# The last block of down: order of its products, place of its transposes, numbering of two PSUM pairs

## The chip, the cores and the metric

The kernel runs on one core of one Trainium2 chip. The metric is the device time of one execution in microseconds (us). Before the change it is 999.88 us, the median of 3 runs (999.58 to 1000.47).

## What is computed

Two residual layers over 512 tokens of 1024 features in float32. Each layer adds a token mixer (layer 0: causal pooling, layer 1: dilated sliding-window attention) and then a SwiGLU; a final rmsnorm follows. What matters here is the SwiGLU and what reads its result:

```python
def swiglu(h, w_gate, w_up, w_down):
    g = jnp.einsum('bsd,df->bsf', h, w_gate)
    u = jnp.einsum('bsd,df->bsf', h, w_up)
    return jnp.einsum('bsf,fd->bsd', jax.nn.silu(g) * u, w_down)

def reference(x, ...):
    for i in range(DEPTH):
        h = rmsnorm(x, norm_mix[i])
        ...
        x = x + y
        h = rmsnorm(x, norm_ffn[i])
        x = x + swiglu(h, ffn_w_gate[i], ffn_w_up[i], ffn_w_down[i])
    return rmsnorm(x, norm_final)
```

`D_FF` is 2816. After layer 0's SwiGLU comes the attention mixer of layer 1; after layer 1's, the final norm and the output.

## The kernel before

Every float32 operand is split into a high part (a cast to float32r on ACT, line 170 for weights: `whi`) and a low part (the rest, a subtraction on DVE, line 174: `wlo`). A product is then three matmuls: high by high, high by low, low by high.

`ffn` computes the SwiGLU with seven products in place of eight (a two-by-two block scheme of Strassen's kind). The features of D_FF are cut into 11 groups (0 to 10) of 256. A group's gate and up come from seven products ("one", "quad"); its activations go into `u_of`. `down` multiplies them with `w_down` in three blocks of groups (`BLOCKS`); the last block, 2, holds groups 6 to 10. In a block, `z` numbers pairs of groups: z = 0 is groups 6 and 7, z = 1 groups 8 and 9, z = 2 group 10 alone. Group 10 keeps its activations in the tiles `t2` and `t3` (high and low; rows of the profile without numbers say `t`), filled in two parts: two slots after quad 10's product 5 (`first_half`), five after its product 6 (`second_half`).

A product of `down` takes, per z, both token halves t and both groups c: 12 matmuls of 512 columns for z = 0 or 1, 6 for z = 2, so 30 in all (line 817). It sums into a pair of PSUM banks. PSUM has four such pairs, opened as `ffpairs`: two that alternate between groups and blocks (list `A`), `Q` (pair2) and `C` (pair3). In block 2, with `accs = (p, r, p, q, p, r, p)`, products 0, 2, 4 and 6 sum into the same pair `p`, 1 and 5 into `r` (which is `C`), 3 into `q` (which is `Q`). Product 0 is copied from `p` to `q` (line 832, ACT) and product 2 is added on top of it. After each product `flush` adds the pair to the residual stream `x` (line 840, DVE) or subtracts it (line 842); only then may the next product on that pair start (0 and 2 share one sum, which starts once). After product 4 the second token block is subtracted once more, for product 6, whose second token block goes to banks of its own.

When both halves of a block of 128 tokens are complete, `closed` squares them (line 323, ACT) and multiplies by the gain (332, DVE); `norm.prepare` scales by the inverse root (338 to 342, then 351 on ACT). After layer 0 the blocks are turned for attention: `turn_block` issues 8 transposes (line 357, PE), then casts (360, ACT) and low parts (361, DVE) into `h`. Blocks 2 and 3 are turned inside `ffn`, into `r` and `q`; the rest in attention. There `by_halves` starts on tiles of a PSUM pool whose four banks are those of the two pairs in `A`, bank 0 first, and needs `h` of blocks 2 and 3 first (lines 263 to 265; features in eight chunks).

PE's order is the order of the code (`manual_schedule`). The other engines' order is set by a scheduler with priorities, statically. Weights go through a queue in the order of `PLAN`: a load on SP's queue into one of 5 `wraw` tiles, in some cases a second one summed onto it by POOL's queue (138, 179), then the split into one of 5 pairs of tiles, up to four items ahead. Products 1, 2 and 5 have no load of their own for all of it: they reuse three `vraw` tiles, and for block 2 the operand of product 5 is that of product 2 plus a POOL DMA (line 179), issued once product 2's split has read the tile.

Of the kernel before, what the change touches and what calls it, by code (L numbers as in the profile page):

```python
# [51 lines left out]
def _plan():  # L52
    first = lambda n: [("quad", n, 0)] if n in PAIRED else []
    down = lambda b, i, *zs: ("down", b, i, zs or tuple(range((len(BLOCKS[b]) + 1) // 2)))
    steps = TWO + [("one", 2, i) for i in range(6)] + first(3) + [("one", 2, 6)]
    for n in PAIRED:
        steps += [("quad", n, i) for i in USED]
        ends = [("quad", n, 5), ("quad", n, 6)]
        if n in (3, 6):
            b = n // 3 - 1  # L60
            steps += [down(b, 0)] + ends + [down(b, i) for i in range(1, 6)] + first(n + 1) + [down(b, 6)]
        elif n == 10:
            steps += [down(2, 0, 0, 1)] + ends + [down(2, 1, 0, 1), down(2, 0, 2), down(2, 1, 2)]
            steps += [down(2, i) for i in (2, 4, 5, 3, 6)]
        else:
            steps += first(n + 1) + ends
    return steps


PLAN = _plan()  # L70
TOKENS = np.arange(S).reshape(J, R).T.reshape(-1)
BY_GROUP = [6, 7, 4, 5, 2, 3, 0, 1]
# [3 lines left out]
def trunk_kernel(ctx: ExitStack, tc: tile.TileContext, x_in, xT, gam, gains, consts, ident_d, w0, wT, w1, wv, w_down, out):  # L76
# [290 lines left out]
    def by_residue(b):  # L367

        n = P // R

        def places(h, half, tp):
            at = h[:, 4 * half : 4 * half + 4, :].rearrange("p c (r j) -> p c r j", r=R)
            return at[:, :, :, b * n : (b + 1) * n], tp.rearrange("p c (i r) -> p c r i", r=R)

        return places

    def turned(norm, shift, b, tps, order):

        hi, lo = tokens_at(shift)
        for half, tp in enumerate(tps):  # L380
            norm.turn(b, half, tp)
        for half, tp in enumerate(tps):
            (to_hi, src), (to_lo, _) = order(hi, half, tp), order(lo, half, tp)
            with tc.high_priority(URGENT):
                split(to_hi, to_lo, src)
# [51 lines left out]
    with ExitStack() as pctx:  # L437
# [64 lines left out]
        v, s, r = (tmp.tile([P, 4], F32, name=name) for name in ("v4", "s4", "r4"))  # L502
# [75 lines left out]
    def ffn(layer, norm, third, nxt):  # L578
# [8 lines left out]
        with ExitStack() as fctx:  # L587
# [193 lines left out]
            def late(b, what):  # L781
                js = slice((b - 2) * P, (b - 1) * P)
                tps = late_banks[b]
                at = lambda t: t[:, :, js]
                parts = lambda i: (at(T_hi[i]), at(T_lo[i]))
                if what == 1:
                    nc.vector.tensor_sub(at(t1r), at(t1r), tps[0])
                    split(*parts(0), at(t1r))
                    nc.scalar.copy(at(t3r), tps[0])
                elif what == 2:  # L790
                    nc.vector.scalar_tensor_tensor(at(t2r), at(t1r), -1.0, tps[1], op0=ALU.mult, op1=ALU.subtract)
                    split(*parts(1), at(t2r))
                elif what == 3:
                    nc.vector.tensor_sub(at(t3r), tps[1], at(t3r))
                    split(*parts(2), at(t3r))
                else:
                    split(at(block(h_hi, 1, 1)), at(block(h_lo, 1, 1)), tps[1])
                    nc.vector.scalar_tensor_tensor(at(t2r), at(t2r), -1.0, at(b21r), op0=ALU.mult, op1=ALU.subtract)
                    split(*parts(3), at(t2r))
# [49 lines left out]
            for at, (kind, n, i, *zs) in enumerate(PLAN[:-4]):  # L849
                if at in (0, 2):  # L850
                    b = 2 + at // 2
                    if b == 2:
                        late_banks[b] = third
                        norm.prepare(3, COLS)
                    else:
                        late_banks[b] = [r_tile(), by_four(mm.tile())]
                        for half in range(2):
                            norm.turn(b, half, late_banks[b][half])
                    late(b, 1)
                if at in (4, 6, 8):  # L860
                    for b in (2, 3):
                        late(b, at // 2)
                if kind == "down":
                    if n not in downs:
                        downs[n] = Down(n, A[0], C, Q)
                        A.reverse()
                    downs[n].product(i, *zs)
                    continue
                if kind == "quad" and i == 0:
                    groups[n] = Group(n, ct_common, (A[0], Q, C))  # L870
                    A.reverse()
                elif i == 0 and n not in groups:
                    groups[n] = Group(n, ct_common)
                groups[n].product(i, held={1: -2, 2: 1, 3: 1}.get(i, 0) if kind == "quad" else 0)
                if (n, i) == (2, 0):
                    with tc.high_priority(100), tc.issue_after(groups[2].kept.ins):
                        groups[1].second_half()
                    held.close()
                    late_u.append(open_pool("ffb", 2))
                if (n, i) == (1, 6):  # L880
                    fps.close()
                    mm.close()
                    fps.open("ffpairs", [P, 2, S], 1)
                    *A, Q, C = (fps.tile(f"pair{i}") for i in range(4))
                    A.reverse()


            final = layer == 1
# [3 lines left out]
            last = downs[2]  # L892
            p, r, _, q = last.accs[:4]

            def closed(half, blocks):
                for b in blocks:
                    norm.square(b, half, junk)
                    norm.gained(b, half)
# [15 lines left out]
            turn_block = lambda b, pair: turned(norm, 0, b, [by_four(pair[:, n, :]) for n in range(2)], by_residue(b))  # L914

            every = PLAN[-1][3]
            last.product(4, every)
            with tc.high_priority(URGENT):
                last.flush(6, p[:, 1:2, :], slice(1, 2))
            closed(1, (2, 3))  # L920
            last.product(5, every)
            closed(0, (2, 3))
            for b in (2, 3):
                ready_block(b)
            last.product(3, every)
            closed(0, (0, 1))
            if not final:
                turn_block(2, r)
            ws = last.operands(6, every)
            last.matmuls(6, ws, last.places(every, (0,)), lambda t: p[:, 0, :], False)  # L930
            with tc.high_priority(URGENT):
                last.flush(6, p[:, 0:1, :], slice(0, 1))
            closed(1, (0,))
            ready_block(0)
            if not final:
                turn_block(3, q)
            for n, cs in enumerate(HALVES if final else COLS[:1]):
                to = (A[0], r)[n][:, 0, : cs.stop - cs.start]
                last.matmuls(6, ws, last.places(every, (1,)), lambda t: to, True, cs)
                with tc.high_priority(URGENT):  # L940
                    last.flush(6, to.unsqueeze(1), slice(1, 2), cs)
                norm.square(1, 1, junk, 2 + n if final else None)
                norm.gained(1, 1, 2 + n if final else None)
# [5 lines left out]
        return norm  # L949

    norm = ffn(0, norm, third, 1)


    with ExitStack() as actx:
# [24 lines left out]
        def rope(ps, t, name):  # L979
            a = aw.tile([P, S], F32, name="ropea")  # L980
            sw = aw.tile([P, S], F32, name="ropeb")
            nc.vector.stream_shuffle(sw, ps, PARTNER)
            nc.vector.tensor_mul(a, ps, cosr)
            nc.gpsimd.tensor_mul(sw, sw, sinr)
            out = aw.tile([P, S], F32, name=name, bufs=3)

            if t >= 3:
                nc.vector.tensor_add(out, a, sw)
            elif name == "k":
                nc.vector.tensor_add(out.rearrange("p (b r i) -> p b r i", b=4, r=R), blocks_of(a), blocks_of(sw))  # L990
            else:
                by_r = lambda z: z.rearrange("p (r j) -> p r j", r=R)
                nc.vector.tensor_add(out.rearrange("p (j r) -> p r j", r=R), by_r(a), by_r(sw))
            return out
# [130 lines left out]
        for t in range(8):  # L1125
            pq = pqk[2 * t] if t < 2 else project(j_qk[2 * t], h_hi, h_lo)
            q = rope(pq, t, "q")
# [4 lines left out]
            if t in (4, 6):  # L1132
                first = (t, q, k)
# [166 lines left out]
        third = out_projection(j_wo, range(NC), m_hi, m_lo, norm, SHIFT, four, lambda: [sc_tile(), sc_tile()])  # L1300

    ffn(1, norm, third, 3)
    mm.close()

# [66 lines left out]
```

## Time and profile before

| | |
|---|---|
| median of 3 runs | 999.88 us |
| profiled execution, its own time | 1001.21 us |
| its span, first to last instruction | 999.4 us |
| mean granted clock of TensorE | 0.996 |
| layer 0, products 1 to 6 of block 2 | PE at 395.7 to 445.4 us |
| layer 1, the same | PE at 945.8 to 993.0 us |

All views show this one execution. A row of the timeline gives start, length, engine, line, operation, out<-in and the idle time ahead of it with what ended it. PEclk is the share of full clock that TensorE was granted. Rows of the windows give, after the stretch and its length, the busy time of PE, PEld, DVE, ACT and POOL, then PEclk, the busy share of the DMA engines and GB/s.

### The profile page before, as it was taken

The numbers are of one execution on the slowest core, as the hardware profiler recorded it, in microseconds if no ns is written. First come the engines' busy times: TensorE is split into PE (matmuls) and PEld (weight loads), VectorE is DVE, ScalarE is ACT, GpSimd is POOL, SyncE is SP. The second block draws the span as 40 slices with busy tenths as digits, with TensorE's granted clock in tenths as the row PEclk, the third lists the DMA queues.
The fourth block names the chain that finished last, engine by engine and source line by source line (L and its number), as shares of the span: only waits on it lengthen the run. The fifth ranks groups of instructions, "written<-read, shape, count | busy, mean of one in ns | idle before, by whom it ended". The sixth has DMA issues, their size and how long they took to land.

```text
span 999.4 us, 15361 instructions
## 1 busy us (share of the span) xinstructions
PE 983.7 (98%) x5914; PEld 871.8 (87%) x5914; DVE 787.0 (79%) x1088; ACT 574.3 (57%) x898; POOL 124.5 (12%) x124
## 2 busy tenths in 40 slices
PE   9999999999999999999999999999999999999997
PEld 8888999989988998779888899899998998899876
DVE  6474889888987888687887547479988898788856
ACT  5573666646755666473443544357664675566545
POOL 0002010011011102001121023101011101110200
PEclk9999999999999999999999999999999999999999
DMA  9457276579479876453211249526757947987642
GB/s 334 177 184 174 64 205 166 141 203 247 113 176 259 200 199 150 108 178 139 76 66 53 61 150 269 111 64 178 186 141 202 253 108 178 262 197 199 153 107 94
DMA packets 79465, 162.98 MB, mean 163 GB/s; under 512 B 6096, under 2 KB 6480, under 8 KB 79392
## 3 DMA queue, kind: packets, MB, share of 16 engines
q1 hardware_dynamic: 58544, 122.04, 36.1%
q0 software_dynamic: 20560, 39.69, 22.9%
q8 instruction: 46, 0.75, 0.3%
q14 instruction: 27, 0.22, 0.1%
q10 hardware_dynamic: 288, 0.27, 0.1%
HBM read 159.85 MB, written 2.13 MB: 162 GB/s over the span
## 4 chain that ended last, share of the span: by engine, by line
PE 94%; ACT 2%; DVE 1%; DMA 1%; issue 1%; POOL 0%; SPq 0%; ACTq 0%; DVEq 0%
PE pair L673 32%; PE pair L817 21%; PE p L699 5%; PE mm L263 4%; PE mm L265 4%; PE mm L264 4%; PE pair L699 4%; PE r L699 2%; PE mm L404 2%; PE mm L402 2%; PE early L484 2%; PE mm L403 2%; PE mm L699 1%; PE early L531 1%; PE tp L1078 1%; ACT e L1004 1%
## 5 line engine op out<-in xcount | busy, mean ns | idle before, releaser
L174 DVE TENSOR_TENSOR wlo<-wraw,whi 128x1024 fp32r<-128x1024 f32 (+2 forms) x190 | 219.8, 1163 | 70.7 <-ACT whi L170 70.1
L170 ACT CAST whi<-wraw 128x1024 fp32r<-128x1024 f32 (+2 forms) x189 | 184.3, 979 | 155.8 <-issue 30.5
L170 ACT CAST whi<-vraw 128x1024 fp32r<-128x1024 f32 (+1 forms) x108 | 105.4, 980 | 122.8 <-PE pair L817 43.9
L174 DVE TENSOR_TENSOR wlo<-vraw,whi 128x1024 fp32r<-128x1024 f32 (+1 forms) x108 | 121.9, 1132 | 52.1 <-ACT whi L170 52.1
L673 PE MATMUL pair<-h,whi 128*128 128x512 f32 (+1 forms) x640 | 143.2, 349 | 0.0
L673 PEld LDWEIGHTS pair<-h,whi 128*128 128x128 f32 x640 | 109.1, 189 | 13.4
L817 PE MATMUL pair<-whi,u_hi 128*128 128x512 f32 (+1 forms) x284 | 111.7, 393 | 5.0 <-DVE x L840 4.6
L817 PE MATMUL pair<-wlo,u_hi 128*128 128x512 f32 (+1 forms) x284 | 111.3, 392 | 0.0
L817 PE MATMUL pair<-whi,u_lo 128*128 128x512 f32 (+1 forms) x284 | 110.9, 391 | 0.0
L673 PE MATMUL pair<-t,whi 128*128 128x512 f32 (+1 forms) x512 | 110.6, 337 | 0.0
L673 PEld LDWEIGHTS pair<-t,whi 128*128 128x128 f32 x512 | 86.0, 190 | 8.4
L673 PE MATMUL pair<-h,wlo 128*128 128x256 f32 x512 | 89.2, 281 | 0.0
L673 PEld LDWEIGHTS pair<-h,wlo 128*128 128x128 f32 x512 | 76.1, 188 | 4.2
L138 POOL DMA_DIRECT2D wraw<-w x22 | 26.6, 1211 | 394.9 <-DMA vraw<-w 76.7
L176 DVE TENSOR_TENSOR vraw<-vraw,wraw 128x1024 f32<-128x1024 f32 (+1 forms) x66 | 75.1, 1138 | 0.7
L673 PE MATMUL pair<-t,wlo 128*128 128x256 f32 x384 | 71.9, 282 | 0.0
L817 PEld LDWEIGHTS pair<-whi,u_hi 128*128 128x128 f32 x284 | 54.1, 190 | 17.2 <-issue 5.4
L263 PE MATMUL mm<-h,whi 128*128 128x512 f32 (+1 forms) x176 | 64.9, 369 | 1.7 <-ACT whi L170 1.7
L817 PEld LDWEIGHTS pair<-whi,u_lo 128*128 128x128 f32 x284 | 54.2, 191 | 11.3
L265 PE MATMUL mm<-h,wlo 128*128 128x512 f32 (+1 forms) x176 | 63.6, 361 | 0.0
L264 PE MATMUL mm<-h,whi 128*128 128x512 f32 (+1 forms) x176 | 63.5, 361 | 0.0
L817 PEld LDWEIGHTS pair<-wlo,u_hi 128*128 128x128 f32 x284 | 54.1, 190 | 10.3
(346 smaller groups left out, 2042.2 us busy)
## 6 DMA issues: line engine op xcount, KB each, us to landing
wraw<-w SPq DMA_DIRECT2D x116, 512.0 KB, 4.7
wraw<-w_down SPq DMA_DIRECT2D x32, 512.0 KB, 4.3
vraw<-w SPq DMA_DIRECT2D x22, 512.0 KB, 4.8
wraw<-w POOLq DMA_DIRECT2D x22, 512.0 KB, 7.3
vraw<-w POOLq DMA_DIRECT2D x22, 512.0 KB, 8.9
wraw<-wT SPq DMA_DIRECT2D x16, 512.0 KB, 4.3
vraw<-w_down POOLq DMA_DIRECT2D x12, 512.0 KB, 5.7
wraw<-w_down SPq DMA_DIRECT2D x24, 256.0 KB, 2.8
```

The source lines that it names most:

```text
L138: nc.gpsimd.dma_start(dst, more, accum_op=ALU.add)
L170: nc.scalar.copy(hi[:, :n], raw[:, :n])
L174: nc.vector.tensor_sub(lo[:, :n], raw[:, :n], hi[:, :n].bitcast(F32))
L176: nc.vector.tensor_add(raws[into][:, :n], raws[into][:, :n], raws[more][:, :n])
L263: nc.tensor.matmul(ps, lhsT=whi, rhs=xhi, start=first, stop=False, **kw)
L264: nc.tensor.matmul(ps, lhsT=whi, rhs=xlo, start=False, stop=False, **kw)
L265: nc.tensor.matmul(ps, lhsT=wlo, rhs=xhi, start=False, stop=last, **kw)
L402: nc.tensor.matmul(ps, lhsT=xhi, rhs=w[0][:, k, :], start=first, stop=False)
L403: nc.tensor.matmul(ps, lhsT=xhi, rhs=w[1][:, k, :], start=False, stop=False)
L673: mat = lambda o, w, m, **kw: nc.tensor.matmul(o, lhsT=w, rhs=m, skip_group_check=True, **kw)
L699: nc.tensor.matmul(ps[:, g, :], lhsT=w[:, g, c, :], rhs=right[:, z, c, :], start=i in (0, 1, 3) and g + c + k == 0, stop=c == 3 and k == 2 ...
L817: nc.tensor.matmul(acc(t), lhsT=u, rhs=w, start=first, stop=n == len(places) - 1, skip_group_check=True)
```

## The change

The order of products in block 2 was 0 (z 0, 1), then quad 10's products 5 and 6, then 1 (z 0, 1), 0 (z 2), 1 (z 2), 2, 4, 5, 3, 6. It becomes 0 (z 0, 1), quad 10's 5 and 6, 1 (z 0), 0 (z 2), 1 (z 1, 2), 2, 5, 4, 3, 6. The two turns move inside product 6: the first behind 12 of its 15 matmuls for the first token block, the second behind 6 of 15 for the second. Without `A.reverse()` the two pairs in `A` change places throughout `ffn`, and product 6's second token block sums into the second bank of its pair.

```diff
         elif n == 10:
-            steps += [down(2, 0, 0, 1)] + ends + [down(2, 1, 0, 1), down(2, 0, 2), down(2, 1, 2)]
-            steps += [down(2, i) for i in (2, 4, 5, 3, 6)]
+            steps += [down(2, 0, 0, 1)] + ends + [down(2, 1, 0), down(2, 0, 2), down(2, 1, 1, 2)]
+            steps += [down(2, i) for i in (2, 5, 4, 3, 6)]
...
                     *A, Q, C = (fps.tile(f"pair{i}") for i in range(4))
-                    A.reverse()
...
             every = PLAN[-1][3]
+            last.product(5, every)
+            closed(0, (2, 3))
             last.product(4, every)
             with tc.high_priority(URGENT):
                 last.flush(6, p[:, 1:2, :], slice(1, 2))
             closed(1, (2, 3))
-            last.product(5, every)
-            closed(0, (2, 3))
             for b in (2, 3):
                 ready_block(b)
             last.product(3, every)
             closed(0, (0, 1))
+            ws = last.operands(6, every)
+            first = last.places(every, (0,))
+            last.matmuls(6, ws, first[:4], lambda t: p[:, 0, :], False)
             if not final:
                 turn_block(2, r)
-            ws = last.operands(6, every)
-            last.matmuls(6, ws, last.places(every, (0,)), lambda t: p[:, 0, :], False)
+            last.matmuls(6, ws, first[4:], lambda t: p[:, 0, :], False)
...
-            if not final:
-                turn_block(3, q)
+            second = last.places(every, (1,))
             for n, cs in enumerate(HALVES if final else COLS[:1]):
-                to = (A[0], r)[n][:, 0, : cs.stop - cs.start]
-                last.matmuls(6, ws, last.places(every, (1,)), lambda t: to, True, cs)
+                to = (A[0], r)[n][:, 1, : cs.stop - cs.start]
+                if final:
+                    last.matmuls(6, ws, second, lambda t: to, True, cs)
+                else:
+                    last.matmuls(6, ws, second[:2], lambda t: to, True, cs)
+                    turn_block(3, q)
+                    last.matmuls(6, ws, second[2:], lambda t: to, False, cs)
```

On PE, layer 0, the end of product 2 (tiles `t2`, `t3`) and the start of the product that follows it (`u_hi`), before and then changed. `pair1` before and `pair0` now are `p`; `pair3` is `r`.

```order
L817 MATMUL pair1_1537<-whi_3861,t2_999 128x512
L817 MATMUL pair1_1537<-wlo_3862,t2_999 128x512
L817 MATMUL pair1_1537<-whi_3861,t3_1000 128x512
L817 MATMUL pair1_1537<-whi_3875,u_hi_2780 128x512
L817 MATMUL pair1_1537<-wlo_3876,u_hi_2780 128x512
```

```order
L817 MATMUL pair0_1536<-whi_3849,t2_999 128x512
L817 MATMUL pair0_1536<-wlo_3850,t2_999 128x512
L817 MATMUL pair0_1536<-whi_3849,t3_1000 128x512
L817 MATMUL pair3_1539<-whi_3875,u_hi_2780 128x512
L817 MATMUL pair3_1539<-wlo_3876,u_hi_2780 128x512
```

The product behind product 2 was on the same pair (4, on `p`) and is now on another (5, on `r`).

On DVE, layer 0, the rows that lead to the low half of group 10's first part (`t3`, line 361), before and then changed. `wlo_3821` and `wlo_3827` are the same low part, of product 2's weights for z = 0; `ct` holds the group's activations.

```order
L742 TENSOR_TENSOR ct_1003<-ct_1003 128x2x256
L652 TENSOR_TENSOR ct_1003<-ct_1003 128x2x256
L174 TENSOR_TENSOR wlo_3821<-vraw_3270,whi_3820 128x1024
L653 SCALAR_TENSOR_TENSOR ct_1003<-ct_1003 128x256
L361 TENSOR_TENSOR t3_1000<-ct_1003,t2_999 128x512
L729 SCALAR_TENSOR_TENSOR ct_1003<-pair0_1536,ct_1003 128x512
```

```order
L742 TENSOR_TENSOR ct_1003<-ct_1003 128x2x256
L174 TENSOR_TENSOR wlo_3827<-vraw_3270,whi_3826 128x1024
L652 TENSOR_TENSOR ct_1003<-ct_1003 128x2x256
L729 SCALAR_TENSOR_TENSOR ct_1003<-pair1_1537,ct_1003 128x512
L653 SCALAR_TENSOR_TENSOR ct_1003<-ct_1003 128x256
L361 TENSOR_TENSOR t3_1000<-ct_1003,t2_999 128x512
```

The low part moved ahead of line 652, and line 729 ahead of 653 and 361.

On ACT, layer 0, the casts around the second turned block (`h` from `pair2`, which is `q`), before and then changed. The casts of line 170 are attention's third, fourth and fifth weight.

```order
L360 CAST h_74<-pair2_1538 128x16x32
L338 ACTIVATE s1_4153<-ss_3919 128x1
L170 CAST whi_4232<-wraw_3992 128x1024
L360 CAST h_74<-pair2_1538 128x16x32
L351 ACTIVATE wraw_3918<-wraw_3918,r1_4154 128x1024
L170 CAST whi_4236<-wraw_4049 128x1024
```

```order
L360 CAST h_74<-pair2_1538 128x16x32
L338 ACTIVATE s1_4153<-ss_3919 128x1
L170 CAST whi_4236<-wraw_4049 128x1024
L170 CAST whi_4241<-wraw_4059 128x1024
L360 CAST h_74<-pair2_1538 128x16x32
L351 ACTIVATE wraw_3918<-wraw_3918,r1_4154 128x1024
```

Between the two halves' casts stood one weight cast, the third; now two stand there, the fourth and the fifth (the third is ahead of the first half).

## The prediction

> **What bounds the kernel now.** I read the page first: the share of each engine and the chain that ended last.
>
> ```profile
> PE 983.7 (98%) x5914; PEld 871.8 (87%) x5914; DVE 787.0 (79%) x1088; ACT 574.3 (57%) x898; POOL 124.5 (12%) x124
> ...
> PE 94%; ACT 2%; DVE 1%; DMA 1%; issue 1%; POOL 0%; SPq 0%; ACTq 0%; DVEq 0%
> ```
>
> TensorE is the bound. The change takes no matmul away, so it can only win what PE loses in waits, and what a wait does to its clock. The second view is therefore who PE waits for, over the whole span:
>
> ```profile
> PE pair L817 <- DVE x L840: 4.6, 2, 2.3
> PE mm L263 <- ACT whi L170: 1.7, 1, 1.7
> ...
> PE pair L357 <- ACT ct L351: 0.8, 1, 0.8
> ...
> PE pair L817 <- ACT pair L832: 0.3, 2, 0.2
> ```
>
> All four kinds lie in or right behind the last block of `down`: the first and the last once per layer, the other two in layer 0 alone. The third view is PE's timeline there, layer 0 and then layer 1. The columns are start, length, and in brackets the idle time and its releaser; a full-clock matmul of 512 columns follows the one before it after 0.23.
>
> ```profile
> 403.70 0.39 PE L817 MATMUL pair<-whi,t 128*128 128x512 f32 x1
> 404.26 0.50 PE L817 MATMUL pair<-whi,u_hi 128*128 128x512 f32 x1 [0.17 <-ACT pair L832]
> 404.60 0.40 PE L817 MATMUL pair<-wlo,u_hi 128*128 128x512 f32 x1
> ...
> 410.96 0.39 PE L817 MATMUL pair<-whi,t 128*128 128x512 f32 x1
> 413.66 0.47 PE L817 MATMUL pair<-whi,u_hi 128*128 128x512 f32 x1 [2.31 <-DVE x L840]
> ...
> 422.18 0.39 PE L817 MATMUL pair<-whi,u_hi 128*128 128x512 f32 x1
> ...
> 428.98 0.39 PE L817 MATMUL pair<-whi,u_hi 128*128 128x512 f32 x1
> ...
> 435.55 0.39 PE L817 MATMUL pair<-whi,t 128*128 128x512 f32 x1
> 436.77 1.09 PE L357 MATMUL pair<-ident,ct 128*128 128x128 f32 x8 [0.83 <-ACT ct L351]
> ...
> 445.20 0.39 PE L817 MATMUL pair<-whi,t 128*128 128x512 f32 x1
> 447.24 0.35 PE L263 MATMUL mm<-h,whi 128*128 128x256 f32 x1 [1.65 <-ACT whi L170]
> ...
> 448.75 0.28 PE L263 MATMUL mm<-h,whi 128*128 128x256 f32 x1
> ```
>
> ```profile
> 961.03 0.39 PE L817 MATMUL pair<-whi,t 128*128 128x512 f32 x1
> 963.73 0.58 PE L817 MATMUL pair<-whi,u_hi 128*128 128x512 f32 x1 [2.31 <-DVE x L840]
> ...
> 972.25 0.39 PE L817 MATMUL pair<-whi,u_hi 128*128 128x512 f32 x1
> ```
>
> Product 2 ends at 410.96 + 0.23 = 411.19. Product 4 accumulates on the same banks, starts at 413.66 and takes until 422.18; product 5, with as many matmuls (30), takes 428.98 − 422.18 = 6.80. So 411.19 to 422.18, 10.99 us, holds 6.80 us of work: **4.19 us lost**. Layer 1 is the same: 972.25 − 961.26 = 10.99. Of the 4.19, 2.47 is the gap and 1.72 is slow matmuls behind it, which the windows show in PEclk (the last column but two):
>
> ```profile
> 400.00:420.00 20.00, 17.51 (x70) 13.69 (x69) 12.18 (x13) 9.44 (x12) 2.11 (x2) 0.91 0.59 131
> ...
> 450.00:950.00 500.00, 499.39 (x3149) 446.23 (x3149) 398.03 (x564) 273.50 (x466) 76.83 (x78) 1.00 0.56 152
> 950.00:970.00 20.00, 17.51 (x70) 13.67 (x69) 12.24 (x13) 9.51 (x12) 2.10 (x2) 0.91 0.59 132
> ```
>
> ```profile
> 415.00:418.00 3.00, 3.00 (x9) 2.36 (x8) 0.00 (x0) 0.00 (x0) 0.00 (x0) 0.53 0.00 0
> ```
>
> Right behind the gap the granted clock is 0.53, where nine matmuls fill three us; between the two gaps, 500 us long, it is 1.00. That is my reason to charge the slow stretch to the gap. (The Trainium skill, "TensorE: Matmul & The Clock Gate", section "What's actually happening", says that the clock halves after at least one idle window of about 3.4 us in a free-running count and comes back after a busy one. The trace agrees with the half rate, but both gaps here are shorter than the window. By that rule the slow stretches would not be the gaps' doing; what the time would be then is the third rival.)
>
> **The change part by part.** The waits for the producers are read from DVE and ACT in layer 0:
>
> ```profile
> 395.91 0.69 DVE L652 TENSOR_TENSOR ct<-ct 128x512 f32<-128x512 f32 x1
> 396.52 1.22 DVE L174 TENSOR_TENSOR wlo<-vraw,whi 128x1024 fp32r<-128x1024 f32 x1
> ...
> 397.99 0.68 DVE L361 TENSOR_TENSOR t<-ct,t 128x512 fp32r<-128x512 f32 x1
> ...
> 402.16 0.69 DVE L174 TENSOR_TENSOR wlo<-vraw,whi 128x512 fp32r<-128x512 f32 x1 [0.32 <-ACT whi L170]
> ...
> 411.16 1.23 DVE L174 TENSOR_TENSOR wlo<-vraw,whi 128x1024 fp32r<-128x1024 f32 x1 [2.33 <-ACT whi L170]
> 412.30 1.22 DVE L840 TENSOR_TENSOR x<-pair,x 128x1024 f32<-128x1024 f32 x1
> ...
> 446.42 0.68 DVE L842 TENSOR_TENSOR x<-x,pair 128x512 f32<-128x512 f32 x1
> ```
>
> ```profile
> 395.06 1.04 ACT L170 CAST whi<-vraw 128x1024 fp32r<-128x1024 f32 x1
> ...
> 396.63 0.62 ACT L360 CAST t<-ct 128x512 fp32r<-128x512 f32 x1
> ...
> 444.55 0.58 ACT L360 CAST h<-pair 128x512 fp32r<-128x512 f32 x1
> ...
> 446.07 1.98 ACT L170 CAST whi<-wraw 128x1024 fp32r<-128x1024 f32 x2
> ```
>
> 1. *Product 5 third.* Product 2's read-out (L840) is behind a low part (L174) on DVE and 1.22 long, so `p` is free only at 413.52. Product 5 writes the other pair, `r`, whose read-out ran during product 2. Product 4 now has product 5's 6.80 us as cover. Both layers: **−4.19 each**. What is late next: on ACT and DVE the read-out now stands behind product 5's third operand and product 4's first. The third operand is summed by a POOL DMA, priced in the first rival. Counted on from product 1's end (404.8): its read-out 1.2, a low part 0.69, 0.4 to the issue, 5.0 to land, casts of 0.6 and 1.0, a low part 1.2, the read-out 1.2, less small overlaps: about 416.3. Product 4 is due at 418.3. Spare: about 1.8 us.
>
> 2. *The first's rest amid the second.* The copy of product 0 (L832) was waited for: from 403.93, when the next matmul was due, the pair of starts 404.26 and 404.60 costs 0.44. It now has 18 matmuls of product 1, 4.1 us, for its 1.00 us of work. Both layers: **−0.44 each**.
>    The six matmuls of product 0 that move forward read the first half of group 10's `t`, and they come 12 matmuls earlier. In the row of DVE that makes it, the low part (L174) now stands ahead of L652. It cannot start before its cast ends, 395.06 + 1.04 = 396.10, and ends 397.36; L652 then ends near 397.98; the cast of `t` on ACT, 0.62, at 398.64; the low half (L361, 0.68) behind L729 and L653 at about 399.54. PE, which starts product 1 at 395.74, would come to the first of the six at 398.46, and to the one that reads the low half at 398.92; it gets there at 399.54 + 0.14 = 399.68. Both layers: **+0.76 each**. Bounds: 0 (no wait stands there before) and 1.22 (the whole low part now ahead). I take 0.76, which uses every row.
>
> 3. *Transposes later* (layer 0 alone). At 436.77 PE lost 436.77 − 435.78 = 0.99 to the row scaling L351. In the change 12 matmuls, 2.72 us, come first, and the scaling comes some 0.7 later (the last closed product now has one more read-out, 0.68, ahead of its squares). 0.99 + 0.7 is below 2.72: **−0.99**. If that cover were gone, the 0.99 would be back.
>
> 4. *Swapped pairs and the start of attention* (layer 0 alone). The last product-6 matmul ends its slot at 445.43; attention starts at 447.24: 1.81 lost. The view names an ACT cast, but L842 at 446.42 ends at 447.10, 0.14 before: it frees bank 0, which attention's first tile takes. With the pairs swapped that bank is free earlier. But the second turned block is now made 6 matmuls later, and its last cast L360 stands behind the fourth and fifth weight casts of attention. The fifth waits for a buffer until product 6 ends. From that end e: two casts (1.98, begun about 0.5 before e) to e + 1.5, L360 0.58, DVE 0.68 (with L842 ahead of it in its queue), and PE gets the low half at e + 3.0. The first four chunks take 448.75 − 447.24 = 1.51, so without a wait that matmul would come at e + 1.6. Cost 1.4 in place of 1.81: **−0.4**. Bounds: 0, and 3.5 (1.81 kept and one slow stretch of 1.72).
>
> Sum: layer 0 −4.19 − 0.44 + 0.76 − 0.99 − 0.4 = −5.26; layer 1 −4.19 − 0.44 + 0.76 = −3.87. Behind product 6 of layer 1, DVE and ACT have the same order as before, so the tail only moves. Together **−9.1 us**: the span of 999.4 becomes 990.3, and the profiled execution's own 1001.21 (1.81 around its span) becomes 992.1. The median shown, 999.88, is 1.33 below that execution; the same 9.1 off it gives **990.8**. The renamed pairs elsewhere change no wait in the order of any engine, and I cost them at nothing.
>
> **The rivals.**
>
> *The wait moves to product 4 (slower).* Product 2's read-out is queued behind product 5's third operand, a POOL DMA:
>
> ```profile
> 403.27 0.89 POOL L179 DMA_DIRECT2D vraw<-w_down  x1 [0.59 <-DVE wlo L174]
> ```
>
> ```profile
> vraw<-w_down POOLq DMA_DIRECT2D x1, 256.0 KB, 5.0
> ...
> wraw<-w_down POOLq DMA_DIRECT2D x1, 256.0 KB, 7.0
> ...
> vraw<-w POOLq DMA_DIRECT2D x22, 512.0 KB, 8.9
> ```
>
> It is issued about 0.4 after its buffer's low part (402.16 + 0.69 = 402.85, then 403.27) and landed in 5.0. With 1.8 us of spare, a landing above 6.8 us holds product 4 up, us for us. At 7.0, the slowest row of this size, it costs 0.2 per layer; at 8.9, the page's slowest group (twice the size), 2.1, hence 995.0. From about 10.5 on, the waits, now over 2.3 us and with the slow stretch behind them, eat the 4.6 us that a layer wins on average; a landing of 11 us (4.2 of waits and 1.72) gives 999.9 − 9.1 + 2 × 5.9 = 1002.6. For it: product 5's operand needs this DMA, and product 4's had long landed. Against it: no landing of this kind in the block is near 10. Chance 0.04 for slower, 0.03 for between 992.5 and the old time.
>
> *A new wait brings a slow stretch.* Attention's start has waits of 1.4 us in two pieces. The 1.81 lost there before brought none, which speaks against it. Price 1.72, at attention's start only: 992.5. Chance 0.10.
>
> *The slow stretches are not the gaps' doing* and stay at these places: 2 × 1.72 of the gain stays out, 994.3. The 500 us at 1.00 between them speak against it; that the two gaps are no longer than 2.47 us speaks for it. Chance 0.07. (This is what the clock rule of the Trainium skill quoted above would make of the time.)
>
> *The change does not do what it says:* the order of the matmuls on PE is shown in the section on the change and does put product 5, on another pair, third. I leave 0.01 for it, at 999.9.
>
> **How the numbers follow.** The forecast, with its bounds to the faster side (two new waits of 0 and no wait at attention: 990.8 − 1.5 − 1.4 = 987.9) and to the slower (two of 1.22: 991.7), has 0.75. The range takes in both and the rivals up to 994.4: attention's upper bound of 3.5 gives 992.9, with both new waits at 1.22 it gives 993.8, and the third rival 994.3. Left out are the first rival's longer landings and the last rival, under 0.1. A measurement of this kernel can tell about 0.2%, 2 us, from no change. Faster by more than that: 0.75 + 0.10 + 0.07 and 0.02 of the first rival = 0.94. Within it: 0.02. Slower: 0.04.
>
> **What would show it.** Right: PE's list of waits has no L840 left; no window of the blocks has PEclk near 0.5; the six matmuls of product 0 wait once per layer, about 0.2 for `t`'s cast and 0.5 for its low half; product 4 follows product 5 without idle time; the first transposes of layer 0 wait for nothing, and attention's first matmuls wait for L361 in place of L842. Wrong: an idle time of over 1 us ahead of product 4 or inside product 5 (the first rival), a slow window without a gap ahead of it (the third), or a wait at a place that none of the steps names.

## Result and profile after

The changed kernel takes **993.51 us** (median of 6 runs, 992.69 to 994.91), the kernel before 1000.17 beside it (6 runs, 999.57 to 1002.1): ratio 0.9933, 95% interval 0.992 to 0.9945. Forecast were 990.8 and a range from 987.9 to 994.4. The profiled execution has a span of 991.4 against 999.4, so 8.0 less, its own time 993.18 against 1001.21.

The page of after, engines and chain:

```profile
PE 981.2 (99%) x5914; PEld 869.8 (88%) x5914; DVE 786.3 (79%) x1088; ACT 573.7 (58%) x898; POOL 124.5 (13%) x124
...
PE 93%; DVE 3%; ACT 2%; DMA 1%; issue 1%; POOL 0%; SPq 0%; DVEq 0%; ACTq 0%
```

Who PE and its weight loads (PEld) wait for, after, in part:

```profile
PEld pair L817 <- DVE t L361: 1.2, 2, 0.6
PE mm L301 <- DVE odd_rows L295: 1.1, 1, 1.1
PE mm L264 <- DVE h L361: 0.9, 2, 0.5
PE mm L1257 <- DVE v L1263: 0.5, 1, 0.5
PE pair L817 <- ACT t L360: 0.4, 2, 0.2
```

L840 with its 4.6 us is gone, and so are L832 and the row scaling L351. New are `t`, once per layer (its cast L360 on PE's rows, its low half L361 on those of the weight loads), and `h` (L361) at attention's start. The windows of after (last columns: PEclk, DMA share, GB/s) have no slow stretch left at the two places:

```profile
400.00:420.00 20.00, 19.90 (x88) 16.49 (x89) 13.65 (x16) 11.86 (x15) 2.11 (x2) 1.00 0.56 113
...
950.00:970.00 20.00, 20.00 (x90) 16.57 (x89) 15.31 (x18) 9.40 (x14) 0.90 (x1) 1.00 0.46 117
```

PE is busy for 19.90 and 20.00 of 20 us, where it was 17.51. The only half clock on record in after's trace is at its end, from 987.28 us, behind the last matmul (984.69). PE's timeline of after, layer 0:

```profile
398.62 0.39 PE L817 MATMUL pair<-whi,u_lo 128*128 128x512 f32 x1
399.22 0.50 PE L817 MATMUL pair<-whi,t 128*128 128x512 f32 x1 [0.21 <-ACT t L360]
399.56 0.40 PE L817 MATMUL pair<-wlo,t 128*128 128x512 f32 x1
400.10 0.73 PE L817 MATMUL pair<-whi,t 128*128 128x512 f32 x2
...
418.60 0.39 PE L817 MATMUL pair<-whi,t 128*128 128x512 f32 x1
418.82 0.39 PE L817 MATMUL pair<-whi,u_hi 128*128 128x512 f32 x1
...
435.15 1.03 PE L357 MATMUL pair<-ident,ct 128*128 128x128 f32 x8
...
441.04 0.28 PE L263 MATMUL mm<-h,whi 128*128 128x256 f32 x1
441.85 0.39 PE L264 MATMUL mm<-h,whi 128*128 128x256 f32 x1 [0.53 <-DVE h L361]
...
443.99 0.39 PE L264 MATMUL mm<-h,whi 128*128 128x256 f32 x1 [0.34 <-DVE h L361]
```

Product 5 ends with the matmul at 418.60, and product 4 follows at 418.82 without idle time; the transposes at 435.15 wait for nothing. Attention's first matmul waits for nothing either, but its second and that of its fifth chunk wait for the low halves of `h`.

Both kernels issue 5914 matmuls on PE. Taking the start of the k-th matmul of before from that of the k-th of after, all along the program, gives each place its share of the difference (us):

| place | predicted | measured |
|---|---|---|
| start of the kernel, first 100 matmuls | 0 | +0.36 |
| layer 0: wait for `t` | +0.76 | +0.93 |
| copy of product 0 | −0.44 | −0.46 |
| product 2 to the third product, gap and clock | −4.19 | −4.18 |
| transposes | −0.99 | −1.05 |
| attention's start | −0.4 | −0.39 |
| attention, later | 0 | +0.48 |
| layer 1: wait for `t` | +0.76 | +0.93 |
| copy | −0.44 | −0.45 |
| product 2 to the third product | −4.19 | −4.19 |
| sum | −9.1 | −8.0 |

In the block and at attention's start the profile gives −8.86 against −9.1. Two questions stay: what the two places outside are, and why the medians fell by only 6.7.

The record of the granted clock points to an answer for the second. In both traces its changes lie on a grid of 3.413 us. The two slow stretches of before are one window each, 549.55 us or 161 windows apart. Windows of before, cut on that grid:

```profile
410.98:414.39 3.41, 1.10 (x5) 0.67 (x4) 3.23 (x3) 1.19 (x2) 0.00 (x0) 1.00 0.51 178
414.39:417.80 3.41, 3.41 (x9) 2.65 (x9) 0.26 (x1) 0.00 (x0) 0.00 (x0) 0.50 0.00 0
960.52:963.94 3.42, 1.11 (x5) 0.64 (x5) 2.72 (x3) 1.72 (x2) 0.00 (x0) 1.00 0.72 265
963.94:967.35 3.41, 3.41 (x9) 2.63 (x9) 0.78 (x1) 0.00 (x0) 0.00 (x0) 0.50 0.00 0
```

Each gap of 2.3 us fell wholly into one window, which left PE 1.10 busy of 3.41; the next window is at half clock. If the grid lies elsewhere in another execution, the same gap is cut in two and may bring no slow window. I call this the grid theory.

### The profile page after: what moved, and what is told of

The parts are those of the page before. It is cut to its first block, busy times and chain, and to the rows that moved or that the text cites. A ratio compares the mean times of both kernels' runs of the same rounds, so it can differ in the third digit from the quotient of the medians.

```text
span 991.4 us, 15359 instructions
## 1 busy us (share of the span) xinstructions
PE 981.2 (99%) x5914; PEld 869.8 (88%) x5914; DVE 786.3 (79%) x1088; ACT 573.7 (58%) x898; POOL 124.5 (13%) x124
## 4 chain that ended last, share of the span: by engine, by line
PE 93%; DVE 3%; ACT 2%; DMA 1%; issue 1%; POOL 0%; SPq 0%; DVEq 0%; ACTq 0%
PE pair L673 31%; PE pair L817 19%; PE p L699 5%; PE mm L263 4%; PE mm L264 4%; PE mm L265 4%; PE pair L699 4%; PE r L699 2%; PE early L484 2%; PE mm L402 2%; PE mm L404 2%; PE mm L403 2%; PE mm L699 1%; DVE wlo L174 1%; PE early L531 1%; PE tp L1083 1%
## 5 line engine op out<-in xcount | busy, mean ns | idle before, releaser
L174 DVE TENSOR_TENSOR wlo<-wraw,whi 128x1024 fp32r<-128x1024 f32 (+2 forms) x190 | 220.1, 1163 | 70.0 <-ACT whi L170 69.5
L174 DVE TENSOR_TENSOR wlo<-vraw,whi 128x1024 fp32r<-128x1024 f32 (+1 forms) x108 | 121.8, 1132 | 44.5 <-ACT whi L170 44.3
```

Source lines behind the costliest of these rows:

```text
L174: nc.vector.tensor_sub(lo[:, :n], raw[:, :n], hi[:, :n].bitcast(F32))
```

## Experiments: the four parts apart

Four kernels each make one part of the change in before; they ran on one chip, with 29 executions of before beside them (median 1001.0).

**Order of products 5 and 4 alone**

```diff
-            steps += [down(2, i) for i in (2, 4, 5, 3, 6)]
+            steps += [down(2, i) for i in (2, 5, 4, 3, 6)]
...
+            last.product(5, every)
+            closed(0, (2, 3))
             last.product(4, every)
```

> Before, with product 5 ahead of product 4 and nothing else changed. The prediction's theory (gap and slow stretch both belong to the wait for product 2's read-out): both waits for L840 go, product 4 follows product 5 without idle time, -4.2 us per layer, -8.4 in the profile; the waits for product 0's copy (L832, 2 x 0.44), for the row scaling (L351, 0.99) and at attention's start (1.81) stay. Rival (slow stretches come on their own): the waits go but a granted clock near 0.5 stays at 411 to 418 and 961 to 968, -2 x 2.47 = -4.9. A second rival, formed from the trace of before: its two slow stretches last 3.413 us each and are 549.55 us apart, 161 times 3.413, so they look like windows of one running grid, and a gap of 2.3 us would bring a slow window only where enough of it falls into one window. By it the profile may show -8.4 or less and the medians of many runs lie between -4.9 and -8.4, near -6.9 with a slow window in some six of ten executions of before.

Measured: 993.82 us, ratio 0.9925 (0.9905 to 0.9945). Both stretches run at full clock now:

```profile
400.00:420.00 20.00, 19.82 (x88) 16.10 (x87) 13.94 (x15) 12.25 (x15) 2.11 (x2) 1.00 0.62 131
950.00:970.00 20.00, 19.82 (x88) 16.08 (x87) 15.01 (x17) 10.42 (x15) 0.90 (x1) 1.00 0.50 120
```

Against before's trace, −4.2 in each layer at this place; both L840 waits and both slow windows are gone. This one swap makes nearly the whole gain. The rival of slow stretches that come on their own is out.

**The first's rest amid the second alone**

```diff
-            steps += [down(2, 0, 0, 1)] + ends + [down(2, 1, 0, 1), down(2, 0, 2), down(2, 1, 2)]
+            steps += [down(2, 0, 0, 1)] + ends + [down(2, 1, 0), down(2, 0, 2), down(2, 1, 1, 2)]
```

> Before, with product 0's rest amid product 1 and nothing else changed. The profile of after had its wait for t at +0.93 and the missing copy wait at -0.45 per layer. If both simply add up: +0.5 per layer, +1.0 in all. If the gap ahead of product 4 (2.31 in before), which ends with work of ACT and DVE, takes up the delay, that gap shrinks by as much and the sum is 0 to +0.3. On the clock: if the gap stays over 2 us, the prediction's theory has a slow window behind each, always; the grid theory has it behind some, both layers of one execution alike or not according to where the gap lies in its 3.413 us window.

Measured: 1000.86 us, ratio 1.0004 (0.9989 to 1.002). By the trace +0.93 for `t` and −0.45 for the copy in each layer; they add up, and the gap behind takes up nothing. The median can't be told from before's. The gap stayed in both layers, but look at PEclk in its windows:

```profile
410.53:413.95 3.42, 1.88 (x9) 1.22 (x7) 1.73 (x2) 2.10 (x2) 0.00 (x0) 1.00 0.95 271
413.95:417.36 3.41, 2.64 (x12) 2.19 (x13) 1.76 (x2) 0.00 (x0) 0.00 (x0) 1.00 0.47 165
417.36:420.77 3.41, 3.41 (x17) 2.83 (x16) 0.69 (x1) 0.91 (x2) 0.00 (x0) 1.00 0.00 0
960.08:963.49 3.41, 1.66 (x8) 1.04 (x6) 1.94 (x2) 2.10 (x2) 0.00 (x0) 1.00 0.94 280
963.49:966.90 3.41, 2.84 (x13) 2.36 (x14) 1.55 (x2) 0.00 (x0) 0.00 (x0) 1.00 0.36 141
```

```profile
414.72 0.47 PE L817 MATMUL pair<-whi,u_hi 128*128 128x512 f32 x1 [2.31 <-DVE x L840]
```

The gap is the same 2.31 us, but a window's edge cuts it, and no slow window follows in either layer. The prediction's theory wanted two. Each layer's matmuls come 1.6 us earlier than in before for that reason alone: this is the price of one slow window (the prediction had 1.72).

**Transposes alone**

```diff
+            ws = last.operands(6, every)
+            first = last.places(every, (0,))
+            last.matmuls(6, ws, first[:4], lambda t: p[:, 0, :], False)
             if not final:
                 turn_block(2, r)
-            ws = last.operands(6, every)
-            last.matmuls(6, ws, last.places(every, (0,)), lambda t: p[:, 0, :], False)
+            last.matmuls(6, ws, first[4:], lambda t: p[:, 0, :], False)
...
+                    last.matmuls(6, ws, second[:2], lambda t: to, True, cs)
+                    turn_block(3, q)
+                    last.matmuls(6, ws, second[2:], lambda t: to, False, cs)
```

> Before, with the transposes of both turned blocks moved into product 6 and nothing else changed; banks not swapped. The wait for the row scaling L351 goes: -0.99 by the prediction, -1.18 as the profile of after has it. Attention's start keeps its wait for bank 0 (L842), which hides part of the later second turned block: together 0 to +0.6 there. Sum -0.4 to -1.2. Layer 1 unchanged. Rival (the later turned block falls wholly on attention, as the prediction's upper bound 3.5 in place of 1.81): +0.5. Slow windows: two by the prediction's theory; none, one or two by the grid theory.

Measured: 1000.2 us, ratio 0.9992 (0.9978 to 1.0005), within what can be told from no change. In the trace the scaling wait is gone (−1.05), and attention's start loses 1.68 instead of 1.81 (−0.12): −1.17 in all, as the first theory has it. Both gaps are there, and only layer 1 has a slow window:

```profile
409.98:413.40 3.42, 2.32 (x11) 1.58 (x9) 1.29 (x2) 2.10 (x2) 0.00 (x0) 1.00 0.91 278
413.40:416.81 3.41, 2.20 (x10) 1.84 (x11) 2.20 (x2) 0.00 (x0) 0.00 (x0) 1.00 0.13 48
...
959.53:962.94 3.41, 1.40 (x7) 0.82 (x5) 2.21 (x2) 2.10 (x2) 0.00 (x0) 1.00 0.84 296
962.94:966.35 3.41, 3.11 (x7) 2.48 (x8) 1.28 (x2) 0.00 (x0) 0.00 (x0) 0.50 0.01 2
```

Layer 0's gap lies half in one window and half in the next; layer 1's leaves 2.0 us of one window idle. One execution with one slow window of two can't come from a rule that looks at the gap's length alone.

**Pairs swapped alone**

```diff
                     *A, Q, C = (fps.tile(f"pair{i}") for i in range(4))
-                    A.reverse()
...
-                to = (A[0], r)[n][:, 0, : cs.stop - cs.start]
+                to = (A[0], r)[n][:, 1, : cs.stop - cs.start]
```

> Before, with the pairs of banks swapped and nothing else changed. Attention's first matmul in before was released by bank 0 (L842 to 447.10) and by its weight cast (446.07 + 0.99 = 447.06) at nearly one time, so freeing the bank alone is worth 0.04: within 0.1 of 0 at that place. Rival (the bank was the only cause): -1.2 or more. Slow windows as for the run before this one.

Measured: 999.56 us, ratio 0.9986 (0.9973 to 1.0), hardly to be told from no change. At the place itself my expectation missed and the rival held. The timeline at attention's start, PE, ACT and DVE:

```profile
444.99 0.39 PE L817 MATMUL pair<-whi,t 128*128 128x512 f32 x1
...
445.21 0.28 PE L263 MATMUL mm<-h,whi 128*128 128x256 f32 x1
...
445.86 1.99 ACT L170 CAST whi<-wraw 128x1024 fp32r<-128x1024 f32 x2
...
446.20 0.68 DVE L842 TENSOR_TENSOR x<-x,pair 128x512 f32<-128x512 f32 x1
...
452.41 1.26 PE L357 MATMUL tp<-ident,odd_rows 128*128 128x128 f32 x8 [0.42 <-DVE h L361]
```

Attention follows product 6 at once: the whole 1.81 are gone. Its first matmul starts 0.65 before the cast that the view of waits had named, so the cast was not what it waited for; in before the two simply ended at the same time. The bank, freed by L842, was the only cause. Of the 1.8 us, 0.8 are lost again by 453 us, where the transposes of another block wait for L361. The slow windows: none in layer 0 (gap cut, 1.59 and 0.72 idle), one in layer 1 (2.31 idle in one window).

**What the eight gaps say.** In the four traces that keep the gap (before, and the three kernels above that keep the old order) it is there eight times, always 2.31 us long. A slow window follows four times, wherever 2.0 us or more of one window are idle (2.01 to 2.31), and never where the larger part is 1.75 or less. (My expectations count from a matmul's slot, 0.16 earlier, hence their 2.17 and 1.91.) Over all 38 executions of before in the two experiments, 18 have a mean granted clock of 0.996 or less, 5 of 0.997, and 15 of 0.998; the median span is 999.6 in the first of these groups and 997.7 in the last. One mean can't count the slow windows of one execution, since the clock is also halved for some of the time behind the last matmul: the trace of before with two has 0.996, and so has that of the swap with one. Taken together they can. The mean over these 38 is 0.9969, and 0.9985 over the 31 executions of the kernels without the gap (the changed one, the swap of products, and the four below). The difference, 0.0016 of 998 us, is 1.6 us of lost clock; a slow window loses 1.7. So an execution of before has 0.9 slow windows of two on average, by this estimate.

## Experiments: waits that the change left

Beside the changed kernel once more, three that mend what it left, on one chip, with 9 executions of before (median 1001.09).

**The changed kernel again** (no edit)

> The changed kernel once more, as the ground for the three runs beside it. By the grid theory (a gap of 2.5 us brings a slow window only if over about 2 us of it, between 1.91 and 2.17 in the runs so far, falls into one window of 3.413 us) it has no slow window in any execution, since its longest waits are near 1 us: the mean granted clock is 0.998 or 0.999 in every run, and its times scatter less than those of before, whose clocks scatter from 0.995 to 0.998. Ratio to before near 0.993. By the prediction's theory before has two slow windows in every execution, and the ratio is 0.991.

Measured: 993.48 us (992.95 to 994.38), ratio 0.9926 (0.9914 to 0.9939). The clock is 0.998 or 0.999 in every execution; that of before was 0.995 to 0.998. The times reach over 1.4 us, before's over 3.2. Against the first trace of the same kernel, the k-th matmuls differ by +0.33 at the start and by −0.63 inside attention, nowhere else by more than 0.05. These two places scatter by themselves, so the +0.36 and +0.48 in the table are no work of the change; the order of PE's matmuls in attention is the same in all these kernels.

**Product 0's rest behind 18 matmuls of product 1** (against after)

```diff
-            steps += [down(2, 0, 0, 1)] + ends + [down(2, 1, 0), down(2, 0, 2), down(2, 1, 1, 2)]
+            steps += [down(2, 0, 0, 1)] + ends + [down(2, 1, 0), down(2, 1, 1), down(2, 0, 2), down(2, 1, 2)]
...
+                    if (n, i) == (2, 1) and zs[0] != (0,):
+                        d, two = downs[n], lambda t: downs[2].accs[1][:, t, :]
+                        if zs[0] == (1,):
+                            kept = d.operands(1, (1,))
+                            d.matmuls(1, kept, d.places((1,), (0,)), two, False)
+                            continue
+                        d.matmuls(1, kept, d.places((1,), (1,)), two, False)
```

> After, with the six matmuls of product 0 behind 18 of product 1 instead of behind 12, so that they come 1.4 us later than after has them. The theory of the wait for t (it costs 0.93 per layer, because the low part of a weight stands ahead on DVE): the wait goes and the copy of product 0 stays covered, -0.9 per layer, -1.8 in all. Rival (the copy L832 has too few matmuls left behind the six and is waited for again): +0.45 per layer against that, -0.9 in all.

Measured: 992.52 us, ratio 0.9911 (0.9898 to 0.9925). In the timeline the six come without a wait:

```profile
399.92 0.39 PE L817 MATMUL pair<-whi,u_lo 128*128 128x512 f32 x1
400.14 0.39 PE L817 MATMUL pair<-whi,t 128*128 128x512 f32 x1
400.37 0.39 PE L817 MATMUL pair<-wlo,t 128*128 128x512 f32 x1
```

Against after's trace this is −0.93 in each layer, and the copy stays covered: the theory holds. The profiled execution loses 2.1 us in attention, 1.8 of that in one wait for L1302. A wait of 1.15 stands at the same place in the last kernel below and none over 0.9 in the other two, so I take it for scatter. The medians differ by 0.96, and the intervals of the two ratios overlap: that the whole 1.86 reach the time is not shown. The wait of 1.82 lies wholly in one window of the grid, and no slow window follows:

```profile
608.92:612.33 3.41, 1.59 (x23) 1.53 (x23) 3.23 (x6) 1.22 (x2) 1.29 (x3) 1.00 0.52 166
612.33:615.75 3.42, 3.42 (x34) 2.87 (x32) 3.24 (x5) 1.24 (x2) 2.03 (x3) 1.00 0.43 153
```

This narrows the grid theory's bound: 1.82 idle us of a window are not enough, 2.01 are. The windows in which PE runs out of work at the end agree in all ten traces: a slow one follows where 2.17 to 2.66 us are idle (five traces), and none where 1.75 or less are (the other five; there it comes one window later, behind a window that is idle throughout).

**Second turned block early, too** (against the kernel just above)

```diff
-                    last.matmuls(6, ws, second[:2], lambda t: to, True, cs)
                     turn_block(3, q)
-                    last.matmuls(6, ws, second[2:], lambda t: to, False, cs)
+                    last.matmuls(6, ws, second, lambda t: to, True, cs)
```

> The kernel before this one, with the second turned block ahead of all of product 6's second token block, where before had it, instead of 6 matmuls into it; the first stays 12 matmuls into the first. The theory: with the pairs swapped alone attention followed product 6 without idle time (-1.81), and in after 1.44 of it came back as the wait for the later block's low half (L361); so here attention's start loses 0 to 0.2 and the kernel is 1.2 to 1.4 faster than the one before it, 3.1 in all against after. Rival (the transposes now wait for the row scaling or for the banks, up to 1.0): -0.4.

Measured: **991.66 us** (4 runs, 990.6 to 992.28), ratio 0.9906 (0.9893 to 0.992). PE around attention's start:

```profile
435.49 1.03 PE L357 MATMUL pair<-ident,ct 128*128 128x128 f32 x8
...
439.56 0.39 PE L817 MATMUL pair<-whi,t 128*128 128x512 f32 x1
439.79 0.28 PE L263 MATMUL mm<-h,whi 128*128 128x256 f32 x1
439.90 0.28 PE L264 MATMUL mm<-h,whi 128*128 128x256 f32 x1
...
447.36 0.93 PE L357 MATMUL tp<-ident,odd_rows 128*128 128x128 f32 x5 [0.54 <-DVE h L361]
```

Neither the transposes nor attention's first matmuls wait now, and 1.25 us are won there. But 0.93 are lost again at 447.4, where another block's transposes wait for L361 as in the kernel with the swap alone: 0.3 net, where I had expected 1.2 to 1.4. That is near the rival's size, but the turned block's transposes wait for neither the row scaling nor the banks. It is the fastest version measured. All of its runs lie below all runs of the changed kernel beside it; the intervals of the two ratios overlap slightly. The trace has 2.6 less than after's (0.3 of it at the start), the medians 1.8.

**Early turn with the old order of products 0 and 1** (against after)

```diff
-            steps += [down(2, 0, 0, 1)] + ends + [down(2, 1, 0), down(2, 0, 2), down(2, 1, 1, 2)]
+            steps += [down(2, 0, 0, 1)] + ends + [down(2, 1, 0, 1), down(2, 0, 2), down(2, 1, 2)]
...
-                    last.matmuls(6, ws, second[:2], lambda t: to, True, cs)
                     turn_block(3, q)
-                    last.matmuls(6, ws, second[2:], lambda t: to, False, cs)
+                    last.matmuls(6, ws, second, lambda t: to, True, cs)
```

> After, with the first's rest as in before (ahead of the second, no wait for t, the copy waited for again) and the second turned block early as in the kernel before this one. The theory: -0.48 per layer for the first (0.93 back, 0.45 lost), -1.3 for the second, -2.3 against after, 0.9 slower than the kernel before this one. Rival as there: -1.4.

Measured: 993.0 us, ratio 0.9917 (0.9905 to 0.9929). By the trace −0.93 and +0.46 per layer for the first part, as expected, and again 1.25 won and 0.92 given back at attention's start. So the places give −1.3 where I had expected −2.3, for the same reason as in the kernel before; the medians differ by only 0.5 from the changed kernel's.

## Why the prediction came out as it did

The sign, the places and the four mechanisms were right; the price of the slow clock was not. 993.51 lies in the range, but 2.7 above the forecast and above the 991.7 up to which the forecast's own bounds went. Only what was added for the rivals and for attention's upper bound, none of which came, takes it in, so that it lies in the range is partly luck.

**Step 1, product 5 third: right in the profile, too large for the medians.** The −4.19 came in the profile as predicted (−4.18 and −4.19). What failed is the reason to charge a slow stretch to every gap. One execution showed it twice, and I took it for the rule. The grid theory, formed from that trace's clock and tested on kernels that keep the gap, has it four times in eight, and the mean clocks give 0.9 of two. Two slow windows at 1.6 us and half the time are 1.6 us less than the prediction took off: −9.1 becomes about −7.5, and −7.3 with all steps as measured (−8.86), against −6.7 and −7.6 in the two comparisons of medians. For the swap of products alone, −8.4 becomes −6.8, against −7.2 (1001.0 to 993.82). That the profiled execution of before was 1.33 above the median of its runs was a sign, and I only subtracted it. What is left, up to 0.6, is of the size by which the start and attention scatter; no run splits it further.

The Trainium skill, "TensorE: Matmul & The Clock Gate", section "What's actually happening", has the clock set by a free-running activity window of 3413 ns; the traces agree, with 3.413 us and an edge that falls elsewhere in each execution. It also asks for at least one idle window before the clock halves. Here the measurement decides: 2.01 idle us of 3.413 were enough, 1.82 were not.

The cover that I priced for product 4 was sufficient. The rows of after on POOL, ACT and DVE:

```profile
407.75 0.89 POOL L179 DMA_DIRECT2D vraw<-w_down  x1 [4.73 <-DVE wlo L174]
...
411.82 0.62 ACT L170 CAST whi<-vraw 128x512 fp32r<-128x512 f32 x1 [2.79 <-DMA vraw<-w_down]
...
414.57 1.22 DVE L840 TENSOR_TENSOR x<-pair,x 128x1024 f32<-128x1024 f32 x1
```

The POOL DMA landed 4.1 us after its issue (5.0 assumed), and the read-out ended at 415.8. Product 4 starts at 418.82: 3.0 spare, where I had about 1.8. So the first rival did not come.

**Step 2: copy right, wait for `t` under-sized.** Its term was 0.76 and it measured 0.93 (by the starts of the matmuls 0.49 up to the cast and 0.44 more up to the low half). DVE and ACT of after:

```profile
396.10 0.68 DVE L742 TENSOR_TENSOR ct<-ct 128x512 f32<-128x512 f32 x1
...
396.70 1.22 DVE L174 TENSOR_TENSOR wlo<-vraw,whi 128x1024 fp32r<-128x1024 f32 x1
397.83 0.68 DVE L652 TENSOR_TENSOR ct<-ct 128x512 f32<-128x512 f32 x1
...
398.55 0.62 ACT L360 CAST t<-ct 128x512 fp32r<-128x512 f32 x1 [1.60 <-DVE ct L652]
399.37 0.68 DVE L361 TENSOR_TENSOR t<-ct,t 128x512 fp32r<-128x512 f32 x1
```

I let the low part (L174) start when its cast ends; but L742 was still ahead of it on DVE, for another 0.2. The low half ended at 400.05, which is 0.15 later than in my chain once the 0.36 of the start is taken off. PE took it up at 400.10, 0.05 behind its end in place of my 0.14, and the next matmul came 0.34 after that one in place of 0.23. Together these are the missing 0.17. Taken alone this part costs more than it saves, and 18 matmuls ahead of product 0's six in place of 12 remove the wait without uncovering the copy.

**Step 3: right.** −0.99 predicted, −1.05 measured, −1.05 alone.

**Step 4: right in sum, and at the wait that ends last.** The wait moved from the bank to the second block's low half, as the prediction had it: 1.81 became 1.42. The fifth chunk got it at 443.99, 2.95 behind product 6's end at 441.04, where I had 3.0. The earlier piece, at the second matmul, adds nothing to that, because the later one ends last. That both parts cannot be added is what the kernels apart show: the swap alone recovers all of the 1.81, and the later turn takes 1.4 of it back.

**The other rivals.** No slow window came at attention's start. The third rival, slow stretches that are not the gaps' doing, is out in its own form: in all ten traces the half clock on record stands behind one of these gaps or behind the last matmul. But its argument, that the gaps were shorter than a window, was the loose thread that led to the grid.

## What to carry to other kernels

When two products in a row share an accumulator, put one with another accumulator between them: here this alone is nearly the whole gain. A slow clock that one profile shows behind a gap shorter than the clock's window (2.31 of 3.413 us here) may be missing in the next execution, so count it at its share over several executions. When the releaser named for a wait ends within hundredths of another event, take that one for a cause as well, and before counting a recovered wait in full, look for the next wait down the line, which here took back 0.8 of 1.8 us in one kernel and 0.9 of 1.25 in another.

## What was unexpected in the hardware

The granted clock halves in whole windows of 3.413 us, and a window that PE left idle for 2.01 us (59%) was enough to make the next one slow, while 1.82 us (53%) was not. The edge of the grid differs between executions of the same program (the first on record is at 4.24 us in one trace of the changed kernel and at 6.84 in the other), so one and the same gap of 2.31 us cost 1.6 us or nothing behind it. With the gaps away, the times of one comparison reached over 1.4 us (5 executions) where before's reached over 3.2 (9); in the first comparison it was 2.2 against 2.5 (6 each), so that the change makes the times steadier is not shown.
